# Two scratch buffers of their own and eight traced steps for the exponent tables of an S5 table builder

## The chip, the cores and the metric

The kernel runs on one core of one Trainium2 chip, as one launch. The metric is the device time of a run in microseconds (us). TensorE (PE) multiplies matrices, VectorE (DVE), ScalarE (ACT) and GpSimd (POOL) work elementwise, and SyncE (SP) issues nearly all DMA transfers, one after the other in the order of its queue: a transfer that has to wait for its data or its buffer holds back all behind it.

## The reference

The kernel computes two layers of a decoder trunk on x, 512 tokens by 1024. A layer is a feed-forward block, a mixer and a second feed-forward block, each between two RMS norms and modulated by a vector made from c. The mixer has gated delta heads and an S5 part. Shortened:

```python
for l in range(2):
    sh1, sc1, gt1, sh2, sc2, gt2, sh3, sc3, gt3 = split(silu(c) @ w_mod[l] + b_mod[l], 9)
    h = modulate(rms_norm(x, ff1_norm_pre[l]), sh1, sc1)
    x = x + 0.5 * gt1 * rms_norm(swiglu(h, ff1_w_in[l], ff1_w_out[l]), ff1_norm_post[l])
    h = modulate(rms_norm(x, mix_norm_pre[l]), sh2, sc2)
    x = x + gt2 * rms_norm(hybrid_mixer(h, ...), mix_norm_post[l])
    h = modulate(rms_norm(x, ff2_norm_pre[l]), sh3, sc3)
    x = x + 0.5 * gt3 * rms_norm(swiglu(h, ff2_w_in[l], ff2_w_out[l]), ff2_norm_post[l])
# S5, per group of 16 channels: a complex diagonal state of 64
abar = exp(dt * min(a_re, -1e-4)) * (cos(dt * a_im) + i sin(dt * a_im))   # dt = exp(log_dt)
x_t = abar * x_(t-1) + bbar * u_t;   y_t = real(c * x_t) + d * u_t
```

The kernel doesn't step the recurrence token by token. It makes tables of powers of the unit-modulus part of abar (er real, ei imaginary, 128 powers for each state) and of the input and output matrices, per layer and for four chunks of channels (4 groups of 128 rows in each table).

## The kernel before, in words

**Weights.** They come from HBM in units of 512 KB (128x1024; DMA on L216, named w0_35 for layer 0, unit 35) into a ring of four raw buffers. Each unit is split on chip into a high and a low half: ScalarE casts (L223, `wh`), VectorE subtracts (L231, `wl`), and three matmuls replace one (L266 to L268 into the hidden layer, tiles f00i, f02i, f10i, f12i; L273 to L275 out of it, f00o and so on: f00 is layer 0's first feed-forward block, f02 its second). A feed-forward block runs in three passes over its 22 hidden tiles: 7, 7 and 8. After a pass its hidden tiles are multiplied out into eight accumulators; L569 adds those of pass 1 on VectorE to the partial sums (f00pt). The second four of these accumulators live in the same PSUM pool as the hidden layer's, so that pass 2 cannot begin on TensorE until L569 has read one.

**The arena.** wh, wl, hidden activations, tables and partial sums all take slots of one pool, 71 buffers of 128x512 in rotation (`slot`, L65); a new tile waits until the last reader of its slot is done.

**Background work.** While a feed-forward block runs, two generators are stepped by a counter at each weight unit (`tick`, L193). `gen_mod` loads a part of w_mod into a raw buffer of the same ring (wm0_53, DMA on L141) and multiplies it on VectorE (L143). `gen_prep` builds the S5 tables, layer 0's beside f00 and layer 1's beside f02. `spread` divides each generator's number of steps over 40 units; for gen_prep it is `NPREP` (L828), 109.

**The table builder.** For each of four chunks (pr00 to pr03, and pr10 to pr13) gen_prep loads parameters (`params`, L692, tile bc, one buffer), computes on GpSimd the input table w, a masked copy (c0r, c0n), the output table c, and then the exponent tables er and ei by doubling: in step i of seven, the 2^i powers at hand are multiplied by the 2^i-th power, which gives the next 2^i (L804 to L818, the products through `pmul`, L679). y1 and y2 hold the products. `close` (L696) then transposes w (L703, pr02mb) and multiplies it (L708, L709, pr02g) on TensorE, and stores everything to a scratch in HBM through SP (L720, L754; er on L725, ei on L726). It runs as part of the next chunk's steps and waits while a pass is being multiplied out. VectorE has one small instruction per chunk, pr03dd (L788), that reads bc.

Order on each engine is that of the trace of the program, except where waits are given: every `yield` of gen_prep is a place where its instructions and the block's own meet, so the number of yields and the rate set which instruction stands before which on every engine.

Of the kernel before, what the change touches and what calls it, by code (L numbers as in the profile page):

```python
# [7 lines left out]
F32 = mybir.dt.float32  # L8
# [3 lines left out]
ALU = mybir.AluOpType  # L12
# [3 lines left out]
P = 128  # L16
# [38 lines left out]
def trunk(ctx: ExitStack, tc: tile.TileContext, x_d, c, wmod, wun, vecs, wab, s5p, cst_d, out, depth=2):  # L55
    nc = tc.nc
    PE, ACT, DVE, POOL = nc.tensor, nc.scalar, nc.vector, nc.gpsimd
# [8 lines left out]
    pw_p = ctx.enter_context(tc.tile_pool(name="prep", bufs=1))  # L66
# [4 lines left out]
    def slot(name, dt=F32):  # L71
        return ar_p.tile([P, T], dt, tag="ar", name=name)

    def small(n, name):
        return sm_p.tile([P, n], F32, tag=f"s{n}", name=name, bufs=NSMALL[n])
# [7 lines left out]
    def q4(t):  # L83
        return t.rearrange("p (c i) -> p c i", c=4)

    def col(t, n):
        return t.rearrange("p (a b) -> p a b", b=1).to_broadcast([P, t.shape[1], n])
# [22 lines left out]
    def rest():  # L110
        behind(nc.scalar.dma_start(out=cst[:, 2 * P:], in_=cst_d[:, 2 * P:]))
        POOL.tensor_copy(identr, ident)
        POOL.tensor_copy(sufr, suf)
        POOL.tensor_copy(negr, cst[:, C_NEG:C_NEG + P])
# [23 lines left out]
    def gen_mod(l, tiles):  # L138
        for n in tiles:
            w = raw_p.tile([P, 1024], F32, tag="raw", name=f"wm{l}_{n}")  # L140
            nc.sync.dma_start(out=w, in_=wmod[l, n])  # L141
            m = small(1, f"ma{l}_{n}")
            DVE.scalar_tensor_tensor(w, w, 1.0, cb, op0=ALU.mult, op1=ALU.mult, accum_out=m)  # L143
            DVE.tensor_tensor(mod[l][:, n:n + 1], m, vec[l][:, V_BMOD + n:V_BMOD + n + 1], op=ALU.add)
            yield
# [43 lines left out]
    def spread(units, **gens):  # L189
        bg.extend([g, n / units, 0.0] for g, n in gens.values())  # L190
# [111 lines left out]
    def new_h(name):  # L302
        return [(slot(f"{name}h{k}", F32R), slot(f"{name}l{k}", F32R)) for k in range(KD)]
# [181 lines left out]
    def ff(l, s, h):  # L485
# [22 lines left out]
        for p, (j0, j1) in enumerate(PASSES):  # L508
            nk = j1 - j0
            js = list(range(j0, j1))  # L510
            if p == 0 and l == 0 and s == 0:
# [5 lines left out]
                rest()  # L517
                spread(40, mod=(gen_mod(0, range(16, 72)), 56), prep=(gen_prep(0), NPREP))
            elif p == 0:
# [55 lines left out]
    def gen_prep(l):  # L575
# [3 lines left out]
        def tiny(nm):  # L579
            return pw_p.tile([P, 16], F32, tag="t" + nm, name=f"t{nm}{l}")  # L580
# [15 lines left out]
        def cm(nm, ar, ai, br, bi):  # L596
            orr, oi = tiny(nm + "r"), tiny(nm + "i")
            mul(t1, ar, br)
            mul(t2, ai, bi)
            sub(orr, t1, t2)  # L600
            mul(t1, ar, bi)
            mul(t2, ai, br)
            add(oi, t1, t2)
            return orr, oi
# [11 lines left out]
        kq, r, z, s, c2, m, ck, sk = [tiny(n) for n in ("kq", "rr", "z", "s", "c", "m", "ck", "sk")]  # L616
# [50 lines left out]
        e = cm("e2", ur, ui, ur, ui)  # L667
        en = [cm("e4", *e, *e)]
# [9 lines left out]
        def pmul(o, a, b):  # L678
            POOL.tensor_tensor(o, a, b, op=ALU.mult)  # L679
# [10 lines left out]
        def params(ch):  # L690
            t = pw_p.tile([P, 384], F32, tag="bc", name=f"pr{l}{ch}bc")
            behind(nc.sync.dma_start(out=t, in_=s5p[l, :, 48 + 384 * ch:432 + 384 * ch]))  # L692
            return t
# [37 lines left out]
        for ch in range(4):  # L731
            qs = slice(4 * ch, 4 * ch + 4)

            def a2(v):
                return col(v[:, qs], 16)

            def q3(v):
                return v.rearrange("p (q h) -> p q h", h=16)

            def part_h(off):  # L740
                return q3(bc[:, off:off + 64])

            def at(v, t):
                return v.rearrange("p (q t h) -> p t q h", q=4, t=4)[:, t]

            def gmask(o, v):
                pmul(o.rearrange("p (q g h) -> p q g h", q=4, g=2),
                     v.rearrange("p q (a h) -> p q a h", a=1).to_broadcast([P, 4, 2, 16]),
                     gm.rearrange("p (a g b) -> p a g b", a=1, b=1).to_broadcast([P, 4, 2, 16]))

            def diag(i, src, ch=ch):
                for g in range(2):
                    v = dram[ch, 64 * g:64 * g + 64, i * T:i * T + T].rearrange("p (q g n) -> p q g n", q=4, g=2)
                    nc.sync.dma_start(out=v[:, :, g], in_=src(g))  # L754

            nm = f"pr{l}{ch}"
            h1 = q3(pw_p.tile([P, 64], F32, tag="k1", name=nm + "k1"))
            h2 = q3(pw_p.tile([P, 64], F32, tag="k2", name=nm + "k2"))

            def step(o_r, o_i, i_r, i_i, m_r, m_i):  # L760
                pmul(h1, i_r, m_r)
                pmul(h2, i_i, m_i)
                POOL.tensor_tensor(o_r, h1, h2, op=ALU.subtract)
                pmul(h1, i_r, m_i)
                pmul(h2, i_i, m_r)
                POOL.tensor_tensor(o_i, h1, h2, op=ALU.add)

            w = slot(nm + "w")
            wr, wi = w[:, 0:256], w[:, 256:512]
            br, bi = part_h(S_BRE), part_h(S_BIM)  # L770
            step(at(wr, 3), at(wi, 3), br, bi, a2(fr), a2(fi))
            yield
            for t in (2, 1, 0):
                step(at(wr, t), at(wi, t), at(wr, t + 1), at(wi, t + 1), a2(a1r), a2(a1i))
                yield
            if rest is not None:
                yield from rest
            c0r = pw_p.tile([P, P], F32, tag="c0r", name=nm + "c0r")
            c0n = pw_p.tile([P, P], F32, tag="c0n", name=nm + "c0n")
            cin = q3(pw_p.tile([P, 64], F32, tag="cin", name=nm + "cin"))  # L780
            gmask(c0r, part_h(S_CRE))
            POOL.tensor_scalar(cin, part_h(S_CIM), -1.0, None, op0=ALU.mult)
            gmask(c0n, cin)
            for _ in range(2):
                yield
            dd = small(P, nm + "dd")
            qg = lambda v: v.rearrange("p (q g h) -> p q g h", q=4, g=2)
            DVE.tensor_tensor(qg(dd[32:64]), qg(bc[32:64, S_D2:S_D2 + P]),  # L788
                              ident[32:64, 48:64].rearrange("p (a b h) -> p a b h", a=1, b=1)
                              .to_broadcast([32, 4, 2, 16]), op=ALU.mult)  # L790
            yield
            yield
            c = slot(nm + "c")
            cr, cn = c[:, 0:256], c[:, 256:512]
            for t in range(4):
                i_r, i_i = (part_h(S_CRE), cin) if t == 0 else (at(cr, t - 1), at(cn, t - 1))
                step(at(cr, t), at(cn, t), i_r, i_i, a2(a1r), a2(nai))
                yield
                if t == 1 and ch < 3:
                    bc = params(ch + 1)  # L800
            er, ei = slot(nm + "er"), slot(nm + "ei")
            POOL.memset(q4(er)[:, :, 0:1], 1.0)
            POOL.memset(q4(ei)[:, :, 0:1], 0.0)
            y1, y2 = slot(nm + "y1"), slot(nm + "y2")  # L804
            for i in range(7):
                n = 1 << i
                z1 = y1[:, :4 * n].rearrange("p (q n) -> p q n", q=4)
                z2 = y2[:, :4 * n].rearrange("p (q n) -> p q n", q=4)
                b_r, b_i = col(en[i][0][:, qs], n), col(en[i][1][:, qs], n)
                lo_r, lo_i = q4(er)[:, :, 0:n], q4(ei)[:, :, 0:n]  # L810
                pmul(z1, lo_r, b_r)
                pmul(z2, lo_i, b_i)
                POOL.tensor_tensor(q4(er)[:, :, n:2 * n], z1, z2, op=ALU.subtract)
                pmul(z1, lo_r, b_i)
                pmul(z2, lo_i, b_r)
                POOL.tensor_tensor(q4(ei)[:, :, n:2 * n], z1, z2, op=ALU.add)
                if i > 3:
                    yield  # L818
            y1 = y2 = z1 = z2 = None
            rest = close(ch, nm, w, c, er, ei, c0r, c0n, dd, qg, diag)  # L820
            w = c = er = ei = wr = wi = cr = cn = c0r = c0n = dd = v = None
            yield
# [2 lines left out]
        yield from rest  # L825

    s5r, s5d, neg = {}, {}, {}
    NPREP = 15 + 4 * 20 + 14  # L828

    def gen_s5(l, utc, res, nm0, chunks):  # L830
        for ch in chunks:
# [688 lines left out]
    h = new_h("h0")  # L1520

    for l in range(depth):
        if l:
            spread(40, mod=(gen_mod(l, range(32, 72)), 40))
        h = ff(l, 0, h)
        drain()
        h = mixer(l, h)
        if l + 1 < depth:
            load_vec(l + 1)
            spread(40, mod=(gen_mod(l + 1, range(32)), 32), prep=(gen_prep(l + 1), NPREP))  # L1530
        h = ff(l, 2, h)
        drain()
# [105 lines left out]
```

## Time and profile before

| | us |
|---|---|
| median of 3 runs | 2133.61 |
| lowest, highest | 2125.81, 2135.41 |
| profiled execution: its own time | 2130.65 |
| span in its profile | 2128.8 |
| TensorE busy | 2040.2 (96% of the span) |
| VectorE, ScalarE, GpSimd busy | 1248.4, 891.9, 489.0 |
| mean granted clock of TensorE, share of full speed | 0.981 |

Times within the span count from its start. The span is the time between the first and the last instruction; the rest of an execution's time lies around it. Busy time overlaps among engines, so that only one engine's idle time can be set against the span. A wait in brackets behind an instruction is the idle time of its engine just before it, and what ended that.

### The profile page before, as it was taken

To read this page: it belongs to the slowest core of one execution; us is meant where nothing else is said; L and a number is where in the kernel's file an instruction comes from. 1 tells how busy PE (TensorE), PEld (TensorE's weight loads), DVE (VectorE), ACT (ScalarE), POOL (GpSimd) and SP (SyncE) were. 2 spreads that over 40 slices of the span, in tenths; PEclk is the share of its full clock that TensorE was granted. 3 is DMA by queue.
4 is the path that set the end of the run, shared out by engine and by line. 5 is a ranking of instruction groups with operands and counts; after the bars stand their busy time and mean duration, and the time that the engine had idled before them with its cause. 6 is when DMAs were issued, how large, how long until landed. Compare 5 with 4: busy or idle time off the path is not lost.

```text
span 2128.8 us, 31850 instructions
## 1 busy us (share of the span) xinstructions
PE 2040.2 (96%) x11702; PEld 1732.1 (81%) x11702; DVE 1248.4 (59%) x2936; ACT 891.9 (42%) x1956; POOL 489.0 (23%) x925
## 2 busy tenths in 40 slices
PE   7999979999999999989999999999989899999998
PEld 5888768798778988868889888888978789888886
DVE  8965556856666864455584456558485575324235
ACT  5532213564567633222363322236637674323132
POOL 4167860211321036663010000001122200000001
PEclk9999989999999999989999999999999899999999
DMA  7776666303311435556423555552142132223231
GB/s 291 234 254 218 208 193 216 109 31 129 116 46 70 149 104 160 169 165 181 153 90 119 165 171 188 162 165 80 30 168 71 41 100 90 93 95 129 70 99 50
DMA packets 109696, 286.07 MB, mean 134 GB/s; under 512 B 31154, under 2 KB 32610, under 8 KB 109540
## 3 DMA queue, kind: packets, MB, share of 16 engines
q1 hardware_dynamic: 108388, 282.39, 40.5%
q8 instruction: 92, 1.51, 0.3%
q10 hardware_dynamic: 1152, 1.65, 0.2%
q14 instruction: 64, 0.52, 0.1%
HBM read 267.59 MB, written 16.41 MB: 133 GB/s over the span
## 4 chain that ended last, share of the span: by engine, by line
PE 72%; DVE 12%; DMA 5%; ACT 4%; issue 3%; POOL 3%; SPq 0%; DVEq 0%; POOLq 0%; ACTq 0%
PE f10i L266 4%; PE f10i L268 4%; PE f10i L267 4%; PE f00i L266 3%; PE f00i L267 3%; PE f12i L268 3%; PE f12i L266 3%; PE f00i L268 3%; PE f12i L267 3%; DMA wm<-in_wmod 3%; PE f02i L266 2%; PE f02i L268 2%; PE f02i L267 2%; DVE wl L231 2%; PE f10o L274 1%
## 5 line engine op out<-in xcount | busy, mean ns | idle before, releaser
L231 DVE TENSOR_TENSOR wl<-w,wh 128x512 fp32r<-128x512 f32 x608 | 408.8, 725 | 105.7 <-ACT wh L223 92.0
L223 ACT CAST wh<-w 128x512 fp32r<-128x512 f32 x648 | 356.7, 617 | 96.6 <-DMA w<-in_wun 50.8
L143 DVE SCALAR_TENSOR_TENSOR wm<-wm,cb 128x1024 f32<-128x1024 f32 x128 | 158.9, 1242 | 224.7 <-DMA wm<-in_wmod 224.6
L266 PE MATMUL f02i<-m0ohh,wh 128*128 128x512 f32 (+1 forms) x416 | 149.7, 362 | 7.9 <-DVE f02pt L569 6.6
L266 PE MATMUL f10i<-f02ohh,wh 128*128 128x512 f32 (+1 forms) x416 | 150.0, 360 | 1.9 <-DVE f02pt L324 1.6
L267 PE MATMUL f10i<-f02ohl,wh 128*128 128x512 f32 (+1 forms) x416 | 148.9, 358 | 2.1 <-ACT f02ohl L404 2.1
L266 PE MATMUL f00i<-h0h,wh 128*128 128x512 f32 x344 | 134.5, 397 | 16.2 <-DVE f00pt L569 12.3
L267 PE MATMUL f02i<-m0ohl,wh 128*128 128x512 f32 (+1 forms) x416 | 149.1, 359 | 0.0
L268 PE MATMUL f02i<-m0ohh,wl 128*128 128x512 f32 (+1 forms) x416 | 148.8, 359 | 0.2 <-DVE wl L231 0.2
L266 PE MATMUL f12i<-m1ohh,wh 128*128 128x512 f32 (+1 forms) x416 | 148.0, 358 | 0.8 <-ACT f12sg L498 0.8
L268 PE MATMUL f10i<-f02ohh,wl 128*128 128x512 f32 (+1 forms) x416 | 148.8, 358 | 0.0
L267 PE MATMUL f12i<-m1ohl,wh 128*128 128x512 f32 (+1 forms) x416 | 148.1, 357 | 0.0
L268 PE MATMUL f12i<-m1ohh,wl 128*128 128x512 f32 (+1 forms) x416 | 147.8, 357 | 0.2 <-DVE wl L231 0.2
L267 PE MATMUL f00i<-h0l,wh 128*128 128x512 f32 x344 | 136.5, 397 | 0.9 <-DVE h0l L1493 0.9
L268 PE MATMUL f00i<-h0h,wl 128*128 128x512 f32 x344 | 135.9, 395 | 0.0
L330 POOL TENSOR_TENSOR f12pt<-f12pt,Gr 128x512 f32<-128x512 f32 x8 | 10.5, 1314 | 403.1 <-ACT scr L329 403.1
L499 DVE TENSOR_TENSOR f12sg<-f12sg,f12i 128x512 f32<-128x512 f32 (+1 forms) x26 | 15.7, 605 | 136.8 <-PE f12i L268 120.8
L266 PEld LDWEIGHTS f02i<-m0ohh,wh 128*128 128x128 f32 x416 | 78.9, 190 | 20.0 <-issue 6.7
L330 POOL TENSOR_TENSOR f10pt<-f10pt,Gr 128x512 f32<-128x512 f32 x8 | 10.7, 1337 | 361.0 <-ACT scr L329 357.2
L266 PEld LDWEIGHTS f10i<-f02ohh,wh 128*128 128x128 f32 x416 | 79.2, 190 | 13.7 <-DVE f02pt L324 1.8
L266 PEld LDWEIGHTS f00i<-h0h,wh 128*128 128x128 f32 x344 | 65.4, 190 | 30.8 <-issue 12.4
L267 PEld LDWEIGHTS f10i<-f02ohl,wh 128*128 128x128 f32 x416 | 79.2, 190 | 13.6 <-ACT f02ohl L404 2.4
(2597 smaller groups left out, 5245.2 us busy)
## 6 DMA issues: line engine op xcount, KB each, us to landing
w<-in_wun SPq DMA_DIRECT2D x324, 512.0 KB, 4.0
wm<-in_wmod SPq DMA_DIRECT2D x128, 512.0 KB, 4.7
wm<-in_wmod SPq DMA_DIRECT2D x32, 256.0 KB, 5.8
s5d<-zero SPq DMA_DIRECT2D x4, 1280.0 KB, 14.6
Gr<-Gd SPq DMA_DIRECT2D x12, 256.0 KB, 3.4
x<-in_x SPq DMA_DIRECT2D x4, 512.0 KB
m0s0tb<-s5d SPq DMA_DIRECT2D x7, 256.0 KB
m0s1tb<-s5d SPq DMA_DIRECT2D x7, 256.0 KB, 4.7
```

Of the source, the lines that this page charges most:

```text
L143: DVE.scalar_tensor_tensor(w, w, 1.0, cb, op0=ALU.mult, op1=ALU.mult, accum_out=m)
L223: ACT.copy(hi[j], raw[:, j * T:j * T + T])
L231: e.tensor_tensor(lo[j], raw[:, j * T:j * T + T], hi[j].bitcast(F32), op=ALU.subtract)
L266: PE.matmul(ps, hi, h[0][:, sl], start=start, stop=False)
L267: PE.matmul(ps, hi, h[1][:, sl], start=False, stop=False)
L268: mark["pe"] = PE.matmul(ps, lo, h[0][:, sl], start=False, stop=stop)
L274: PE.matmul(ps, gh, lo, start=False, stop=False)
L330: (POOL if self.part else DVE).tensor_tensor(y, src, self.G[dh], op=ALU.mult)
L499: DVE.tensor_tensor(sg, sg, pu[:, :n], op=ALU.mult)
```

## The change

y1 and y2 become two tiles of 128x128 with a buffer of their own each, in the pool `prep`, in place of two arena slots of 128x512. So that they suffice, the last doubling step (i=6) works on two of the four groups at a time: twelve GpSimd instructions of 128x128 products in place of six of 128x256. The steps end after i=0, 1, 3, 4, 5 and each half of 6, and once more as before: eight in place of four per chunk, and NPREP goes from 109 to 125, so that more steps are made at each weight unit.

```diff
--- before.py
+++ after.py
@@ -801,21 +801,22 @@
             er, ei = slot(nm + "er"), slot(nm + "ei")
             POOL.memset(q4(er)[:, :, 0:1], 1.0)
             POOL.memset(q4(ei)[:, :, 0:1], 0.0)
-            y1, y2 = slot(nm + "y1"), slot(nm + "y2")
+            y1, y2 = [pw_p.tile([P, P], F32, tag=f"y{i}", name=f"{nm}y{i}") for i in range(2)]
             for i in range(7):
                 n = 1 << i
-                z1 = y1[:, :4 * n].rearrange("p (q n) -> p q n", q=4)
-                z2 = y2[:, :4 * n].rearrange("p (q n) -> p q n", q=4)
-                b_r, b_i = col(en[i][0][:, qs], n), col(en[i][1][:, qs], n)
-                lo_r, lo_i = q4(er)[:, :, 0:n], q4(ei)[:, :, 0:n]
-                pmul(z1, lo_r, b_r)
-                pmul(z2, lo_i, b_i)
-                POOL.tensor_tensor(q4(er)[:, :, n:2 * n], z1, z2, op=ALU.subtract)
-                pmul(z1, lo_r, b_i)
-                pmul(z2, lo_i, b_r)
-                POOL.tensor_tensor(q4(ei)[:, :, n:2 * n], z1, z2, op=ALU.add)
-                if i > 3:
-                    yield
+                for h in ((slice(0, 2), slice(2, 4)) if i == 6 else (slice(0, 4),)):
+                    m = h.stop - h.start
+                    z1, z2 = [y[:, :m * n].rearrange("p (q n) -> p q n", q=m) for y in (y1, y2)]
+                    b_r, b_i = [col(e[:, 4 * ch + h.start:4 * ch + h.stop], n) for e in en[i]]
+                    lo_r, lo_i = q4(er)[:, h, 0:n], q4(ei)[:, h, 0:n]
+                    pmul(z1, lo_r, b_r)
+                    pmul(z2, lo_i, b_i)
+                    POOL.tensor_tensor(q4(er)[:, h, n:2 * n], z1, z2, op=ALU.subtract)
+                    pmul(z1, lo_r, b_i)
+                    pmul(z2, lo_i, b_r)
+                    POOL.tensor_tensor(q4(ei)[:, h, n:2 * n], z1, z2, op=ALU.add)
+                    if i != 2:
+                        yield
             y1 = y2 = z1 = z2 = None
             rest = close(ch, nm, w, c, er, ei, c0r, c0n, dd, qg, diag)
             w = c = er = ei = wr = wi = cr = cn = c0r = c0n = dd = v = None
@@ -825,7 +826,7 @@
         yield from rest
 
     s5r, s5d, neg = {}, {}, {}
-    NPREP = 15 + 4 * 20 + 14
+    NPREP = 15 + 4 * 24 + 14
 
     def gen_s5(l, utc, res, nm0, chunks):
         for ch in chunks:
```

The number of instructions grows by 48 on GpSimd (6 for each of eight chunks) and is the same on every other engine, where the order changes. Three places follow. In the rows w_35_2302 is unit 35 of the weights (the last number is only the tile's), and wm_43 a part of w_mod.

SP's queue, layer 0, around the stores of pr01er and pr01ei. Before:

```order
L141 DMA wm_42_2234<-in_wmod 128x1024
L754 DMA s5d<-pr01c 64x4x64 x2
L216 DMA w_35_2302<-in_wun 128x1024
L141 DMA wm_43_2312<-in_wmod 128x1024
L141 DMA wm_44_2317<-in_wmod 128x1024
L725 DMA s5d<-pr01er 128x512
L726 DMA s5d<-pr01ei 128x512
L216 DMA w_36_2378<-in_wun 128x1024
L141 DMA wm_45_2388<-in_wmod 128x1024
L720 DMA s5d<-pr01gs 16x64 x2
```

And now:

```order
L216 DMA w_34_2236<-in_wun 128x1024
L754 DMA s5d<-pr01c 64x4x64 x2
L141 DMA wm_42_2246<-in_wmod 128x1024
L725 DMA s5d<-pr01er 128x512
L726 DMA s5d<-pr01ei 128x512
L216 DMA w_35_2314<-in_wun 128x1024
L141 DMA wm_43_2324<-in_wmod 128x1024
L141 DMA wm_44_2329<-in_wmod 128x1024
L216 DMA w_36_2390<-in_wun 128x1024
L141 DMA wm_45_2400<-in_wmod 128x1024
```

The two stores have moved ahead of w_35, wm_43 and wm_44. Further on pr03bc moves from behind w_40, w_41 and three stores of pr02c to a place ahead of w_40; around the stores of pr02er and pr02ei nothing moves.

VectorE, layer 0, at the end of f00's pass 1, where f00gl_2377 and w_38 are operands of the multiplication out of the hidden layer. Before:

```order
L159 SCALAR_TENSOR_TENSOR G_1_4828<-mod_124,vec_122 128x8
L499 TENSOR_TENSOR f00sg_2478<-f00sg_2478,f00i_2453 128x512
L501 TENSOR_TENSOR f00gl_2377<-f00sg_2478,f00gh_2376 128x512
L231 TENSOR_TENSOR wl_0_2493<-w_38_2487,wh_0_2489 128x512
L231 TENSOR_TENSOR wl_1_2494<-w_38_2487,wh_1_2490 128x512
L231 TENSOR_TENSOR wl_0_2527<-w_39_2521,wh_0_2523 128x512
L231 TENSOR_TENSOR wl_1_2528<-w_39_2521,wh_1_2524 128x512
L788 TENSOR_TENSOR pr03dd<-pr03bc,cst 32x128
L231 TENSOR_TENSOR wl_0_2561<-w_40_2555,wh_0_2557 128x512
```

And now:

```order
L159 SCALAR_TENSOR_TENSOR G_1_4852<-mod_124,vec_122 128x8
L788 TENSOR_TENSOR pr03dd<-pr03bc,cst 32x128
L499 TENSOR_TENSOR f00sg_2498<-f00sg_2498,f00i_2473 128x512
L501 TENSOR_TENSOR f00gl_2389<-f00sg_2498,f00gh_2388 128x512
L231 TENSOR_TENSOR wl_0_2513<-w_38_2507,wh_0_2509 128x512
L231 TENSOR_TENSOR wl_1_2514<-w_38_2507,wh_1_2510 128x512
L231 TENSOR_TENSOR wl_0_2547<-w_39_2541,wh_0_2543 128x512
L231 TENSOR_TENSOR wl_1_2548<-w_39_2541,wh_1_2544 128x512
L231 TENSOR_TENSOR wl_0_2581<-w_40_2575,wh_0_2577 128x512
```

pr03dd, which reads pr03bc, has moved ahead of f00sg, f00gl and the units 38 and 39.

TensorE, layer 0, between pass 1 (f00o) and pass 2 (f00i) of f00. Before:

```order
L274 MATMUL f00o_2618<-wl_1_2578,f00gh_2376 128x512
L275 MATMUL f00o_2618<-wh_1_2574,f00gl_2377 128x512
L162 MATMUL Gp_0_2836<-cst,G_0_2834 8x128
L703 MATMUL pr02mb_2877<-cst,pr02w 64x128 x4
L703 MATMUL pr02mb_2883<-cst,pr02w 64x128 x4
L708 MATMUL pr02g<-pr02c0r,pr02w 64x32
L709 MATMUL pr02g<-pr02c0n,pr02w 64x32
L708 MATMUL pr02g<-pr02c0r,pr02w 64x32
L709 MATMUL pr02g<-pr02c0n,pr02w 64x32
```

And now (the rows of f00i at the top are the end of the first hidden tile's first unit in pass 2):

```order
L266 MATMUL f00i_2893<-h0h_119,wh_1_2654 128x512
L267 MATMUL f00i_2893<-h0l_120,wh_1_2654 128x512
L268 MATMUL f00i_2893<-h0h_119,wl_1_2658 128x512
L703 MATMUL pr02mb_2940<-cst,pr02w 64x128 x4
L703 MATMUL pr02mb_2946<-cst,pr02w 64x128 x4
L708 MATMUL pr02g<-pr02c0r,pr02w 64x32
L709 MATMUL pr02g<-pr02c0n,pr02w 64x32
L708 MATMUL pr02g<-pr02c0r,pr02w 64x32
L709 MATMUL pr02g<-pr02c0n,pr02w 64x32
```

The small matmuls of pr02 stood before the first matmul of pass 2 and now stand behind its first 24.

## Rows read from the trace of the kernel before

**Rows 1.** The page's first part: busy time, share of the span and instructions.

```profile
PE 2040.2 (96%) x11702; PEld 1732.1 (81%) x11702; DVE 1248.4 (59%) x2936; ACT 891.9 (42%) x1956; POOL 489.0 (23%) x925
```

**Rows 2.** Busy time by stretch: PE, PEld, DVE, ACT, POOL; then TensorE clock, DMA share, GB/s.

```profile
240.00:260.00 20.00, 20.00 (x90) 16.57 (x89) 12.26 (x23) 2.28 (x4) 17.23 (x42) 1.00 0.72 241
260.00:280.00 20.00, 4.00 (x34) 3.27 (x33) 8.75 (x18) 4.42 (x9) 18.12 (x42) 0.69 0.53 160
280.00:300.00 20.00, 20.00 (x79) 16.37 (x80) 10.71 (x18) 3.91 (x7) 17.45 (x53) 0.89 0.47 146
940.00:960.00 20.00, 10.42 (x49) 8.26 (x48) 13.33 (x25) 3.43 (x8) 11.78 (x30) 0.67 0.51 168
```

**Rows 3.** The waits: total us, times, longest.

```profile
ACT wh L223 <- POOL pr02ei L816: 15.6, 1, 15.6
...
ACT wh L223 <- POOL pr12ei L816: 13.2, 1, 13.2
```

**Rows 4.** Timeline of TensorE, 255 to 285: start, length, what ran, [idle before].

```profile
261.63 0.27 PE L162 MATMUL Gp<-cst,G 128*8 128x128 f32 x1
261.74 1.03 PE L703 MATMUL pr02mb<-cst,pr02w 128*64 128x128 f32 x8
266.46 0.27 PE L708 MATMUL pr02g<-pr02c0r,pr02w 128*64 128x32 f32 x2 [3.69 <-DVE f00pt L569]
...
267.27 0.28 PE L709 MATMUL pr02g<-pr02c0n,pr02w 128*64 128x32 f32 x2
279.87 0.77 PE L266 MATMUL f00i<-h0h,wh 128*128 128x512 f32 x1 [12.31 <-DVE f00pt L569]
```

**Rows 5.** Timeline of VectorE, 256 to 285.

```profile
264.23 1.49 DVE L231 TENSOR_TENSOR wl<-w,wh 128x512 fp32r<-128x512 f32 x2 [8.78 <-ACT wh L223]
...
269.50 1.22 DVE L143 SCALAR_TENSOR_TENSOR wm<-wm,cb 128x1024 f32<-128x1024 f32 x1 [1.63 <-DMA wm<-in_wmod]
...
277.69 1.23 DVE L143 SCALAR_TENSOR_TENSOR wm<-wm,cb 128x1024 f32<-128x1024 f32 x1 [3.51 <-DMA wm<-in_wmod]
...
279.04 2.47 DVE L569 TENSOR_TENSOR f00pt<-f00pt,f00o 128x512 f32<-128x512 f32 x4
```

**Rows 6.** Timeline of SP's DMA queue, 255 to 285.

```profile
261.51 0.33 SPq L725 DMA_DIRECT2D s5d<-pr02er  x1
...
265.74 2.29 SPq L141 DMA_DIRECT2D wm<-in_wmod  x2
...
274.02 0.33 SPq L141 DMA_DIRECT2D wm<-in_wmod  x1
```

**Rows 7.** Timeline of GpSimd, 225 to 285.

```profile
240.85 0.33 POOL L679 TENSOR_TENSOR pr03k<-pr03bc,tfr 128x64 f32<-128x64 f32 x1 [4.00 <-DMA pr03bc<-in_s5p]
...
256.74 0.40 POOL L679 TENSOR_TENSOR pr02y<-pr02er,te128r 128x128 f32<-128x128 f32 x1
...
259.48 0.61 POOL L679 TENSOR_TENSOR pr02y<-pr02er,te256r 128x256 f32<-128x256 f32 x1
...
263.50 0.32 POOL L763 TENSOR_TENSOR pr03w<-pr03k,pr03k 128x64 f32<-128x64 f32 x1
```

**Rows 8.** Timeline of SP's DMA queue, 920 to 960.

```profile
928.74 0.33 SPq L726 DMA_DIRECT2D s5d<-pr12ei  x1
929.15 0.38 SPq L216 DMA_DIRECT2D w<-in_wun  x1
```

**Rows 9.** Timeline of TensorE, 935 to 960.

```profile
955.04 0.77 PE L266 MATMUL f02i<-m0ohh,wh 128*128 128x512 f32 x1 [6.61 <-DVE f02pt L569]
```

**Rows 10.** Timeline of SP's DMA queue, 195 to 252.

```profile
202.87 0.33 SPq L216 DMA_DIRECT2D w<-in_wun  x1
...
220.70 0.53 SPq L216 DMA_DIRECT2D w<-in_wun  x1
```

**Rows 11.** Timeline of VectorE, 225 to 256.

```profile
226.94 1.50 DVE L231 TENSOR_TENSOR wl<-w,wh 128x512 fp32r<-128x512 f32 x2
...
240.74 0.28 DVE L788 TENSOR_TENSOR pr03dd<-pr03bc,cst 32x128 f32<-32x128 f32 x1 [5.72 <-DMA pr03bc<-in_s5p]
```

## The prediction

> **What bounds the kernel now.** I read the page first: TensorE is busy for 2040.2 of the span's 2128.8 us [rows 1], so at most 88.6 us are idle and a change pays only where TensorE stands still, or where it makes it stand still. Next came the busy time by stretches of 20 us. TensorE fills nearly every one (20.00), and around the table builder two do not: 4.00 us in 260 to 280, with a granted clock of 0.69, and 10.42 in 940 to 960, with 0.67 [rows 2]. I call them stall A (layer 0) and stall B (layer 1). Then the waits: ScalarE's cast L223 waits 15.6 us once for GpSimd's pr02ei on L816, and 13.2 us once for pr12ei [rows 3]. The casts want an arena slot that the doubling's scratch y1 or y2 still holds. These waits look like the whole story; the timelines say less.
>
> In stall A TensorE finishes f00o at 261.63, does two pieces of small table matmuls (pr02mb 1.03 us, pr02g 0.8 from its first start to its last) and starts f00i14 at 279.87, after 12.31 us for L569 [rows 4]. VectorE's own rows show what L569 stood behind: wl44 after 8.78 us for the cast, then four modulation products L143, of which the later ones wait for their loads wm (1.63 us, and 3.51 the last), then L569 at 279.04 [rows 5]. Why are the loads late? The DMA queue of SP is in order: the store of pr02er leaves at 261.51, w0_46 behind it, wm0_53 and wm0_54 from 265.74 (into a raw buffer that wl44 frees), then the store of pr02ei, w0_47 and, at 274.02, wm0_55 [rows 6]. So two things hold stall A, and both end with GpSimd's doubling: the slot (pr02ei complete at 263.5) and the store that blocks SP (pr02er, which it takes up at 261.51) [rows 6, 7].
>
> In stall B the slot's wait ends at 928.7, but SP stands at the store of pr12ei until 928.74 too, and issues w0_138 at 929.15 only [rows 8]. TensorE resumes at 955.04, after 6.61 us for L569 [rows 9]. The slot and the queue are released by one and the same instruction.
>
> **The change, part by part.** *Own buffers.* The waits of L223 and L231 for pr02ei and pr12ei go. What is late next is SP. In stall A, wl44 no longer comes after the doubling, so wm0_53 and wm0_54 follow the store of pr02er at once instead of 4.2 us later (265.74 less 261.51). From there I repeat the old pace. A load is consumed 3.7 us after its issue (274.02 to 277.69 [rows 5, 6]), and a product with its readout takes 1.3. Call T the end of pr02er. wm0_53 is issued at T+0.8, its product runs from 4.5 to 5.8, wm0_54's from there to 7.1, wm0_55 is issued at 7.2, its product ends at 12.2, and one L569 later (0.95 us from the product's end to 279.87) f00i14 starts, at T+13.2. Before, 279.87−261.51=T+18.4. That is −5.2 us if T stays.
>
> *T itself.* The doubling step i=5 takes 259.48−256.74=2.74 us for six 128x128 operations, step i=6 263.50−259.48=4.02 for six of 128x256 [rows 7]. Two halves of i=6 cost 2x2.74, +1.46 per chunk. pr02er's last write was the third of six (261.51−259.48=2.0 us into the step) and is now the ninth of twelve (4.1): +2.1. The chunk before is on the way too: +1.46. Against this, pr03bc is now loaded before w0_40 instead of after it, w0_41 and three stores, so GpSimd's wait of 4.00 us for it [rows 7] can go entirely. Sum −0.4. pr02bc moves ahead of wm0_39, worth up to about a load's 3.7 us earlier, while more of pr01's doubling stands behind it: I bound this by ±4 and take T about 1 us earlier in all, the sum's side. f00i14 then starts at 260.5+13.2=273.7 instead of 279.87, −6.2.
>
> *Matmuls that move.* pr02mb and pr02g stood inside the stall, where they cost nothing. In the new order they follow f00i14's first unit, whose cover is gone: 1.03+0.8=+1.8 [rows 4]. **Stall A: −4.4 us**, between −8 and 0.
>
> *Stall B.* The order around pr12 is as before. SP still stops at pr12er and pr12ei, whose doubling ends 1.46 us later, and everything from w0_138 to 955.04 follows. Taking away ACT's and VectorE's wait gives nothing, since the next operand is still to be issued. **+1.5 us**, between −3 (wl137 earlier frees a buffer that is used early) and +2.
>
> *SP's order.* The stores of pr01er and pr01ei now precede w0_35 to w0_37 instead of following w0_35. w0_35 left at 202.87 and will wait for pr01ei, about 213; w0_37 left at 220.70 and I put it at about 227.6 [rows 10]. It is needed when f00o's fifth row of pass 1 begins, at 261.63−120x0.222=235.0 (120 matmuls before its end, 90 of them in 20.00 us [rows 2]). Its wl followed its issue by 7.7 us before (220.70 to 228.44 [rows 10, 11]), so 235.3: at the edge. *pr03dd* on VectorE, which waited 5.72 us for pr03bc [rows 11], now stands ahead of f00sg13, f00gl13 and wl38, which TensorE needs about 235.8. pr03bc then lands near 237 and wl38 is ready near 239.5: a new stall of some 4 us. I cost it at nothing, because it only moves f00o's end from 261.6 towards 266, and stall A ends at 273.7 whatever f00o does. If stall A were gone, these 4 us would count in full. The same move in pr00 and in layer 1's pr10, pr11 and pr13 puts stores in front of loads that ran about 10 us ahead; zero, between 0 and +2. The 48 additional GpSimd instructions otherwise lie beside matmuls.
>
> Sum: −4.4+1.5+0=−2.9 on the profiled execution's own 2130.65 (span 2128.8 plus 1.9 around it), 2127.8. That execution lies 3.0 under the median of 2133.61, so the median comes to about 2131.
>
> A page of the Trainium skill argues for more. "Perfetto Trace Analysis", section Optimization Strategy, says that a repeated gap on the engine that should be saturated can mean too little SBUF for the next tile. By it both stalls would be gaps of the arena. The rows agree that a slot is waited for [rows 3], and show beside it a queue that is released at the same moment [rows 6, 8]. By the page the sum would be the first rival's time below, by the rows the one above.
>
> **Rivals.** *The slots were the cause.* If the arena alone made the loads late, since slots free the raw buffers and so SP, the whole run of loads moves forward. Stall A's 12.31+3.69 and stall B's 6.61 of waiting go [rows 4, 9], and with them the clock's loss (0.69 and 0.67 in these stretches). The rows for it are the waits [rows 3]; against it stand SP's stores, which wait for GpSimd in any order [rows 6, 8]. Price: −16 (A alone) to −27 (A, B, and 2 us each for matmuls that come back slowly: 79 start in the 20 us after stall A instead of 90 [rows 2]). About 2112.
>
> *Stores before weights* (the other side). Each microsecond by which pr03bc or pr01's tables come later delays T and f00sg13 by one. SP reaches pr03bc only after w0_35 to w0_39, whose issue hangs on pr01ei. From T of about 264.9, 3.4 us above today's (the 5.2 gained less 1.8), each further microsecond is one on the time. With pr03bc landing at 252 instead of 240.7, T is near 273, f00i14 near 286: +6 there, +1.8 matmuls, +1.5 in B and 2 to 5 from starved passes in layer 1: +11 to +14, about 2146. For it: SP's order and 17 to 18 us of work in every 20 on GpSimd [rows 2]. Against: w0_37's load had 6 us in hand before (ready 228.44, needed 235.0).
>
> *Nothing moves.* If T grows by the 3.4, A is unchanged, and the time is the old one within B's +1.5: 2135.
>
> **How the numbers follow.** The forecast, a small gain, 0.47, with its own range 2125 to 2137. Slots the cause 0.22, nothing moves 0.14, stores before weights 0.17. About 10.7 us (0.5%) can be told from no change here. Faster by more takes the first rival and a little of the forecast: 0.24. Slower by more takes the second: 0.16. Within: 0.60. For 8 in 10 the range takes half of each outer rival: 2113 to 2145.
>
> **What would show it.** In the changed profile the waits for pr02ei and pr12ei are gone; SP's store of pr02er leaves near 260.5 with wm0_53 right behind; f00i14 starts near 274 with pr02mb after its first unit; VectorE waits for pr03bc near 232 to 237 and f00o has a gap there; f02i14 of layer 1 starts some 13 us after f02o's end, as now. I am wrong if SP's stores of pr02er and pr12er leave 5 us or more from there, or if 940 to 960 fills up.

## The result, and the profile after

The changed kernel takes 2146.28 us (median of 5 runs, 2142.01 to 2148.05) against 2131.86 of the kernel before beside it. The ratio is 1.0065, with a 95% interval of 1.005 to 1.008: slower by some 14 us, where about 2131 had been forecast. Its profiled execution took 2146.28 us with a span of 2144.5, 15.7 more than the one of before.

First the page's line of busy time, which answers to [rows 1]:

```profile
PE 2045.4 (95%) x11702; PEld 1733.0 (81%) x11702; DVE 1243.4 (58%) x2936; ACT 892.0 (42%) x1956; POOL 509.4 (24%) x973
```

TensorE has the same 11702 matmuls in 5 us more (the mean granted clock is 0.977 instead of 0.981), so some 10 us of the 15.7 are idle time. Then the stretches of 20 us that answer to [rows 2]:

```profile
200.00:220.00 20.00, 18.44 (x96) 15.02 (x94) 7.45 (x15) 3.34 (x7) 17.75 (x44) 1.00 0.35 109
220.00:240.00 20.00, 9.51 (x32) 7.29 (x33) 11.48 (x20) 5.81 (x11) 18.02 (x41) 0.66 0.63 196
260.00:280.00 20.00, 16.75 (x75) 13.54 (x73) 10.38 (x20) 2.40 (x5) 18.06 (x39) 0.99 0.50 172
280.00:300.00 20.00, 9.10 (x32) 7.25 (x32) 9.08 (x18) 1.33 (x3) 6.23 (x15) 0.58 0.55 183
```

There are two holes beside layer 0's tables now, a new one from 218 to 230, and stall A, which has moved from 262 to 280 to 276 to 291. TensorE's timeline, the first matmul after each hole, and after stall B (for [rows 4, 9]):

```profile
230.49 0.79 PE L266 MATMUL f00i<-h0h,wh 128*128 128x512 f32 x1 [12.05 <-ACT wh L223]
```

```profile
290.90 0.76 PE L266 MATMUL f00i<-h0h,wh 128*128 128x512 f32 x1 [14.15 <-DVE f00pt L569]
```

```profile
969.89 0.76 PE L266 MATMUL f02i<-m0ohh,wh 128*128 128x512 f32 x1 [6.40 <-DVE f02pt L569]
```

f00i14, with which pass 2 of f00 begins, starts at 290.90 instead of 279.87, +11.0. f02i14, the same place in f02 (the second block of layer 0, beside which layer 1's tables are built; the prediction calls it layer 1), starts at 969.89 instead of 955.04, +14.9. Nearly all of the loss is there. SP's queue, around the stores of pr01 and of pr02 (for [rows 6, 10]):

```profile
204.36 0.33 SPq L141 DMA_DIRECT2D wm<-in_wmod  x1
218.33 0.33 SPq L725 DMA_DIRECT2D s5d<-pr01er  x1
219.70 0.33 SPq L726 DMA_DIRECT2D s5d<-pr01ei  x1
220.13 0.37 SPq L216 DMA_DIRECT2D w<-in_wun  x1
```

```profile
275.65 0.33 SPq L725 DMA_DIRECT2D s5d<-pr02er  x1
276.03 0.42 SPq L216 DMA_DIRECT2D w<-in_wun  x1
276.56 0.87 SPq L141 DMA_DIRECT2D wm<-in_wmod  x2
...
284.54 0.33 SPq L141 DMA_DIRECT2D wm<-in_wmod  x1
```

SP issues nothing between 204.7 and 218.33: it stands at the store of pr01er. w0_35 leaves at 220.13 instead of 202.87. The store of pr02er leaves at 275.65 instead of 261.51. GpSimd's waits for the parameters and for the slot of pr02ei (for [rows 7]), and VectorE's for the loads behind SP's stops (for [rows 5]):

```profile
196.06 0.39 POOL L679 TENSOR_TENSOR pr02k<-pr02bc,tfr 128x64 f32<-128x64 f32 x1 [11.62 <-DMA pr02bc<-in_s5p]
```

```profile
247.30 0.33 POOL L679 TENSOR_TENSOR pr03k<-pr03bc,tfr 128x64 f32<-128x64 f32 x1 [4.23 <-DMA pr03bc<-in_s5p]
...
251.83 0.10 POOL L803 MEMSET pr02ei<- 128x4 f32 x1 [3.57 <-DMA s5d<-pr02c]
```

```profile
226.09 1.23 DVE L143 SCALAR_TENSOR_TENSOR wm<-wm,cb 128x1024 f32<-128x1024 f32 x1 [15.69 <-DMA wm<-in_wmod]
```

```profile
281.94 1.23 DVE L143 SCALAR_TENSOR_TENSOR wm<-wm,cb 128x1024 f32<-128x1024 f32 x1 [10.98 <-DMA wm<-in_wmod]
...
288.73 1.23 DVE L143 SCALAR_TENSOR_TENSOR wm<-wm,cb 128x1024 f32<-128x1024 f32 x1 [4.02 <-DMA wm<-in_wmod]
...
290.08 2.48 DVE L569 TENSOR_TENSOR f00pt<-f00pt,f00o 128x512 f32<-128x512 f32 x4
```

### The profile page after: what moved, and what is told of

Read it like the earlier page. It is cut to its first block, busy times and chain, and to the rows that moved or that the text cites. A ratio compares the mean times of both kernels' runs of the same rounds, so it can differ in the third digit from the quotient of the medians.

```text
span 2144.5 us, 31901 instructions
## 1 busy us (share of the span) xinstructions
PE 2045.4 (95%) x11702; PEld 1733.0 (81%) x11702; DVE 1243.4 (58%) x2936; ACT 892.0 (42%) x1956; POOL 509.4 (24%) x973
## 4 chain that ended last, share of the span: by engine, by line
PE 62%; DVE 14%; DMA 8%; POOL 6%; issue 4%; ACT 4%; SPq 1%; DVEq 0%; POOLq 0%; ACTq 0%
DMA wm<-in_wmod 5%; PE f10i L266 4%; PE f10i L267 4%; PE f10i L268 4%; PE f12i L268 3%; PE f12i L266 3%; PE f12i L267 3%; DVE wl L231 2%; PE f02i L266 2%; PE f02i L268 2%; PE f02i L267 2%; PE f00i L266 1%; PE f00i L268 1%; PE f00i L267 1%; PE f12o L273 1%
## 5 line engine op out<-in xcount | busy, mean ns | idle before, releaser
L231 DVE TENSOR_TENSOR wl<-w,wh 128x512 fp32r<-128x512 f32 x608 | 405.7, 720 | 99.8 <-ACT wh L223 98.4
L223 ACT CAST wh<-w 128x512 fp32r<-128x512 f32 x648 | 356.8, 618 | 109.9 <-DMA w<-in_wun 75.6
L499 DVE TENSOR_TENSOR f12sg<-f12sg,f12i 128x512 f32<-128x512 f32 (+1 forms) x26 | 15.7, 606 | 136.8 <-PE f12i L268 120.8
```

The lines of the kernel that those rows point to most:

```text
L223: ACT.copy(hi[j], raw[:, j * T:j * T + T])
L231: e.tensor_tensor(lo[j], raw[:, j * T:j * T + T], hi[j].bitcast(F32), op=ALU.subtract)
L499: DVE.tensor_tensor(sg, sg, pu[:, :n], op=ALU.mult)
```

## The experiments

Two numbers are followed through all of them: T, the end of pr02er on GpSimd, and the start of f00i14 on TensorE. Both are read from one profiled execution of each kernel. A third is the ratio to the kernel before run beside each kernel.

| kernel | scratch | last doubling | steps | bc loads | T | f00i14 | f00i14 − T | ratio, 95% interval |
|---|---|---|---|---|---|---|---|---|
| before | arena | 6 | 4 | SP | 261.5 | 279.87 | 18.4 | |
| e6_own_unsplit | own | 6 | 4 | SP | 261.5 | 277.24 | 15.7 | 0.9992 [0.9981, 1.0004] |
| e9_split_arena | arena | 12 | 4 | SP | 266.0 | 283.88 | 17.9 | 1.0060 [1.0041, 1.0079] |
| e1_four_steps | own | 12 | 4 | SP | 268.6 | 283.57 | 15.0 | 1.0043 [1.0027, 1.0059] |
| e2_eight_steps_arena | arena | 6 | 8 | SP | 267.8 | 286.93 | 19.1 | 1.0032 [1.0020, 1.0045] |
| e12_own_unsplit_eight | own | 6 | 8 | SP | 269.3 | 284.45 | 15.2 | 1.0017 [1.0005, 1.0028] |
| after | own | 12 | 8 | SP | 275.6 | 290.90 | 15.3 | 1.0065 [1.0050, 1.0080] |
| e10_after_bc | own | 12 | 8 | GpSimd | 266.4 | 281.73 | 15.3 | 0.9963 [0.9951, 0.9975] |
| e8_before_bc | arena | 6 | 4 | GpSimd | 251.9 | 270.95 | 19.0 | 0.9913 [0.9898, 0.9928] |
| e7_own_unsplit_bc | own | 6 | 4 | GpSimd | 254.2 | 269.79 | 15.6 | 0.9905 [0.9890, 0.9920] |

**Order or work?** Two kernels take the change apart: one has the four steps back, the other has only the eight steps.

```diff
 # e1_four_steps, against the changed kernel
-                    if i != 2:
+                    if i > 3 and h.stop == 4:
                         yield
-    NPREP = 15 + 4 * 24 + 14
+    NPREP = 15 + 4 * 20 + 14
 # e2_eight_steps_arena, against the kernel before
-                if i > 3:
+                if i != 2:
+                    yield
+                if i == 6:
                     yield
-    NPREP = 15 + 4 * 20 + 14
+    NPREP = 15 + 4 * 24 + 14
```

> Own scratch buffers and the split last doubling stay; the steps are four per chunk again (NPREP 109), so that every engine but GpSimd has the order of the kernel before. Theory O (the eight steps' order does the harm: stores of pr01er and pr01ei ahead of w0_35 hold SP, and pr02's parameters come behind more of pr01's doubling): no stall near 218, SP's store of pr01er within 4 us of 208, f00i14 starts between 273 and 280, time 2126 to 2134. Theory W (the 48 additional GpSimd instructions, +1.46 us per chunk, make the tables late): the store of pr02er leaves 4 us or more after 261.5, f00i14 at 283 or later, time 2138 or more.

> The kernel before (scratch in the arena, last doubling in six instructions) with eight steps per chunk and NPREP 125: SP, TensorE and ScalarE have the order of the changed kernel. Theory O: the stall near 218 is there with about 12 us, time 2142 to 2152 (a little more than the changed kernel if the arena's waits for pr02ei add to it). Theory W: no such stall, time 2130 to 2137.

Neither theory held alone. e1 took 2140.51 us against 2130.45, as W says, with SP's and TensorE's order of before; e2 took 2136.17, a time that W allows, but with the early hole (the one near 218) that only O foresees, of 7.24 us instead of 12. SP's store and f00i14 in e1, and the two matmuls behind the holes of e2:

```profile
268.63 0.33 SPq L725 DMA_DIRECT2D s5d<-pr02er  x1
```

```profile
283.57 0.76 PE L266 MATMUL f00i<-h0h,wh 128*128 128x512 f32 x1 [19.12 <-DVE f00pt L569]
```

```profile
225.62 0.79 PE L266 MATMUL f00i<-h0h,wh 128*128 128x512 f32 x1 [7.24 <-ACT wh L223]
```

```profile
286.93 0.77 PE L266 MATMUL f00i<-h0h,wh 128*128 128x512 f32 x1 [14.38 <-DVE f00pt L569]
```

T is 7.1 us later in e1 and 6.3 later in e2; both together make 13.4, and the changed kernel has 14.1. f00i14 is later by 3.7 and 7.1, together 10.8; the changed kernel has 11.0. The parts add up, and they act through T.

**SP's stop at the stores.** Two kernels send er and ei through GpSimd's own queue: e3 is the changed kernel with this edit, e5 is e1 with it.

```diff
-            nc.sync.dma_start(out=dram[ch, :, 5 * T:6 * T], in_=er)
-            nc.sync.dma_start(out=dram[ch, :, 6 * T:7 * T], in_=ei)
+            nc.gpsimd.dma_start(out=dram[ch, :, 5 * T:6 * T], in_=er)
+            nc.gpsimd.dma_start(out=dram[ch, :, 6 * T:7 * T], in_=ei)
```

> The changed kernel with the stores of er and ei issued by GpSimd's own DMA queue, so that SP never waits for the doubling; orders are else the same but for a few swaps. If SP standing at these stores is the cause (theory O, its first half): w0_35 leaves near 204, the 12 us near 218 go, and most of the 14 us at f00i14 too, time 2112 to 2126. If instead GpSimd is late because pr02's parameters land late and its work lies behind that wait (second half), DVE's and TensorE's waits move to pr03bc and the slots: f00i14 near 285, time 2135 or more.

> Own scratch buffers, four steps, and the stores of er and ei on GpSimd's queue: both things that hold stalls A and B in the kernel before (slot, and SP behind the stores) are taken away, in its order. My reading of the two stalls: f00i14 starts by 268 instead of 279.87 and f02i14 by 947 instead of 955.04, time 2108 to 2120. If the modulation loads are late for another reason (the raw ring alone): f00i14 at 275 or later, time 2126 or more.

e3 took 2134.35 us (ratio 1.0016, 1.0006 to 1.0026). The early hole was gone, so SP's stop at pr01er had made it; and T was 264.6, 11 us earlier, with 2.39 us for pr02bc instead of 11.62, as SP now reached that load sooner. But f00i14 still started at 284.85, as the second half of its expectation had it. e5 missed by 15 us: 2135.39 (1.0017, 1.0005 to 1.0029), with f00i14 at 287.27. TensorE's row in e3, and VectorE's row in e5, which shows what took SP's place:

```profile
284.85 0.76 PE L266 MATMUL f00i<-h0h,wh 128*128 128x512 f32 x1 [20.76 <-DVE f00pt L569]
```

```profile
269.18 0.71 DVE L231 TENSOR_TENSOR wl<-w,wh 128x512 fp32r<-128x512 f32 x1 [11.35 <-DMA s5d<-pr02er]
```

wl44, the other half of the unit whose cast waited for y1 or y2 before, now waits for an arena slot that the store of pr02er frees (10.35 us in e3). The raw buffers wait with it: w0_46 leaves at 271.39 in e5, when wl44 is done. er and ei lie in the arena too, so that one wait for a slot is followed by the next. In e5 y1 and y2 are out of the arena and SP is free; what is left is the last of three waits that end with the same doubling.

**Scratch, split and steps one by one.** e6 has own scratch alone: one buffer of 128x256, the second product going straight into its place; e9 the split of the last doubling alone (the changed loop, y1 and y2 from the arena, steps and NPREP of before); e12 is e6 with the eight steps of e2.

```diff
 # e9_split_arena, against the changed kernel (with the steps of e1_four_steps)
-            y1, y2 = [pw_p.tile([P, P], F32, tag=f"y{i}", name=f"{nm}y{i}") for i in range(2)]
+            y1, y2 = slot(nm + "y1"), slot(nm + "y2")
 # e6_own_unsplit, against the kernel before
-            y1, y2 = slot(nm + "y1"), slot(nm + "y2")
+            y1 = pw_p.tile([P, 2 * P], F32, tag="y0", name=f"{nm}y0")
...
-                pmul(z2, lo_i, b_i)
-                POOL.tensor_tensor(q4(er)[:, :, n:2 * n], z1, z2, op=ALU.subtract)
+                pmul(hi_r, lo_i, b_i)
+                POOL.tensor_tensor(hi_r, z1, hi_r, op=ALU.subtract)
```

> The kernel before with one scratch buffer of its own (128x256 floats, the second product goes straight into its place in er or ei), four steps, the last doubling in six instructions: own scratch alone, without the split and without the eight steps. Theory S (the split's additional GpSimd time, added up chunk after chunk, is what e1_four_steps lost): the store of pr02er leaves at 260 to 264 and f00i14 starts 15 us after it, at 275 to 279; time 2124 to 2132. If own scratch itself costs (the slots turn in another order), f00i14 is at 281 or later and the time 2136 or more.

> The split alone: scratch in arena slots, four steps, the last doubling in twelve instructions. Theory S: pr02er is done near 268 as in e1_four_steps, f00i14 starts 18 to 19 us later, at 286 to 288, f02i14 about 2 us later again than that shift; time 2138 to 2145, the worst of the four with four steps. If the split costs nothing: 2128 to 2134.

> The changed kernel without the split: one scratch buffer of its own (128x256), the last doubling in six instructions, eight steps; SP, TensorE, VectorE and ScalarE have exactly the order of the changed kernel. If split and eight steps add up: pr02er is done near 268 as in e2_eight_steps_arena, the stall near 218 to 226 has 6 to 8 us, f00i14 starts 15 to 16 us after pr02er, at 282 to 285, time 2130 to 2138, half of the changed kernel's loss. If the eight steps do all of the harm: 2142 or more, with 11 us or more near 218. If the split does all: 2125 to 2130.

The three came out as expected, but that e9's T was 266.0 instead of 268, and its f00i14 2 us earlier with it; its f02i14 (964.12) lay 9 us behind that of before, 5 more than f00i14, where 2 more were expected. Own scratch alone: 2127.56 us, f00i14 2.6 us earlier at the same T, in all no more than the measurement can tell. Split alone: 2140.44. Own scratch and eight steps: 2133.96, with an early hole of 6.71 us. From e12 to the changed kernel the split is added (and the one scratch buffer becomes two), and on every engine but GpSimd the order is the same: 1.0017 to 1.0065, some 10 us. So the split costs 10 to 13 us with eight steps as with four (e6 to e1, 0.9992 to 1.0043; e9 alone, 1.0060), and the eight steps about 5 (e6 to e12). SP's store and f00i14 in e6, and the two matmuls behind the holes of e12:

```profile
261.56 0.33 SPq L725 DMA_DIRECT2D s5d<-pr02er  x1
```

```profile
277.24 0.77 PE L266 MATMUL f00i<-h0h,wh 128*128 128x512 f32 x1 [13.20 <-DVE f00pt L569]
```

```profile
225.04 0.79 PE L266 MATMUL f00i<-h0h,wh 128*128 128x512 f32 x1 [6.71 <-ACT wh L223]
```

```profile
284.45 0.77 PE L266 MATMUL f00i<-h0h,wh 128*128 128x512 f32 x1 [13.09 <-DVE f00pt L569]
```

How long does the split step take? The last doubling step took 6.1, 5.0 and 4.1 us in chunks 0 to 2 before, and 7.6, 8.2 and 5.4 in e1: 6.0 us more in all, where three times 1.46 would be 4.4. In the changed kernel it took 5.43 in each of the three, and in e12, without the split, 3.95: there the split cost no more than its own work. GpSimd's rows of the first of these in e1, and VectorE's:

```profile
155.02 0.40 POOL L679 TENSOR_TENSOR pr00y<-pr00er,te256r 128x128 f32<-128x128 f32 x1
155.38 1.44 POOL L679 TENSOR_TENSOR pr00y<-pr00ei,te256i 128x128 f32<-128x128 f32 x1
...
157.43 0.40 POOL L679 TENSOR_TENSOR pr00y<-pr00er,te256i 128x128 f32<-128x128 f32 x1
```

```profile
155.33 1.23 DVE L143 SCALAR_TENSOR_TENSOR wm<-wm,cb 128x1024 f32<-128x1024 f32 x1 [1.75 <-DMA wm<-in_wmod]
```

The same product takes 0.40 us, and 1.44 where it meets a modulation product of VectorE's; it ends 0.26 us after that one. "SBUF — State Buffer", section SBUF: two separate sides, of the Trainium skill says that VectorE, with two inputs from SBUF, and GpSimd share a pair of ports as an exclusive lock for a whole instruction. The rows agree; no run here took VectorE's work away to show it.

**How the chunks hang together.** A longer doubling in one chunk reaches the next through SP's queue, where bc stands behind the stores of er and ei of the chunk before. SP's rows in the kernel before, and in e1:

```profile
157.20 0.33 SPq L725 DMA_DIRECT2D s5d<-pr00er  x1
...
188.44 0.38 SPq L692 DMA_DIRECT2D pr02bc<-in_s5p  x1
```

```profile
161.32 0.33 SPq L725 DMA_DIRECT2D s5d<-pr00er  x1
...
191.02 0.38 SPq L692 DMA_DIRECT2D pr02bc<-in_s5p  x1
```

The stores of pr00er and pr00ei leave 4.1 and 2.3 us later in e1, and pr02bc 2.6; those of pr01 4.8 and 4.2, and pr03bc 3.1. The one buffer of bc is not what holds the load: in e1 GpSimd had read pr01bc for the last time at 173.7.

**The chain on GpSimd.** If T is what counts, GpSimd's waits for bc should be worth as much as its work. They are taken out by loading bc through GpSimd's queue:

```diff
-            behind(nc.sync.dma_start(out=t, in_=s5p[l, :, 48 + 384 * ch:432 + 384 * ch]))
+            behind((nc.gpsimd if ch else nc.sync).dma_start(out=t, in_=s5p[l, :, 48 + 384 * ch:432 + 384 * ch]))
```

> The kernel before with only the bc loads moved to GpSimd's queue. If GpSimd's chain sets the stalls: pr02er's store by 253, f00i14 by 275 (the slot of y1 and y2 holds it 3 us longer than own scratch), time 2108 to 2122. If not: 2126 or more.

> As e6_own_unsplit, and the parameters bc of chunks 1 to 3 are loaded through GpSimd's own DMA queue instead of SP's, behind the instructions that free the buffer. If GpSimd's chain from one chunk to the next sets the stalls: its waits for pr02bc and pr03bc (7.9 and 4.0 us) shrink to under 3 us together, the store of pr02er leaves by 253, stall A is under 10 us and f00i14 starts by 272; in layer 1 the waits for pr12bc and pr13bc (8.7, 16.7) go and f02i14 starts 8 to 13 us earlier; time 2106 to 2120. If the chain isn't what sets them, 2126 or more.

> The changed kernel with the bc loads of chunks 1 to 3 on GpSimd's queue; split and eight steps stay. If the chain on GpSimd is what both act through: the wait of 11.6 us for pr02bc goes, pr01er is done by 210 and SP's store of it no longer starves TensorE near 218, pr02er is done by 264, f00i14 starts by 279; time 2112 to 2126. If the eight steps hurt by SP's order alone, w0_35 still leaves 8 us or more later than in the kernel before, the stall near 218 stays, time 2130 or more.

> e7_own_unsplit_bc with the stores of er and ei on GpSimd's queue as well, four steps: nothing of the tables holds SP. Where the slots of er and ei are what is left (as the 11.35 us for the store of pr02er in e5_four_steps_pool_stores), f00i14 starts 13 to 18 us after pr02er, no earlier than in e7 (269.8), time 2106 to 2113. If SP's stop at the stores was still the larger part, f00i14 starts by 266 and the time is 2100 to 2106.

e8 took 2110.89 us, e7 2108.58, e10 2122.44: the change of one queue gains some 18 us on the kernel before (0.9913) and 22 on the changed one (1.0065 to 0.9963). In e10 the wait for pr02bc went from 11.6 to 0.98 us, pr01er was done at 209.1, and the early hole shrank to 2.41; the split and the eight steps are still in it, and T (266.4) and f00i14 came 2.5 us after the bounds I had set. In e10 w0_35 still left at 212.05, 9.2 us later than before, as the other expectation had it, but neither the long hole nor the time that it tied to this came. The rows of e7: GpSimd's issue of pr03bc and its wait for it, which did not go as expected, SP's store, a little after the 253 expected, and f00i14.

```profile
224.72 0.59 POOL L692 DMA_DIRECT2D pr03bc<-in_s5p  x1
230.14 0.72 POOL L679 TENSOR_TENSOR pr03k<-pr03bc,tfr 128x64 f32<-128x64 f32 x1 [4.83 <-DMA pr03bc<-in_s5p]
```

```profile
254.24 0.33 SPq L725 DMA_DIRECT2D s5d<-pr02er  x1
```

```profile
269.79 0.77 PE L266 MATMUL f00i<-h0h,wh 128*128 128x512 f32 x1 [4.88 <-DVE f00pt L569]
```

On GpSimd's queue pr03bc is issued as the last instruction ahead of its own first use, so that GpSimd waits for the whole load, though the buffer had been read for the last time at 213.35. Beside f02 the wait for pr13bc fell from 16.66 us before to 3.40, and f02i14 started without a wait of over 1 us, at 936.44 instead of 955.04, more than the 8 to 13 us expected: stall B is gone. e11, with the stores on GpSimd's queue as well, took 2112.96 us (0.9921, 0.9903 to 0.9940): no better than e7, the slot of er again (VectorE waits 9.39 us for its store). That is the first of the two expectations, but f00i14, at 275.29, came 21.7 us after T, as in e5, and not 13 to 18. e7 beats both kernels, by 0.95% and 1.6%.

## Why the prediction was wrong

**The step that failed is T.** The prediction put it at 260.5, "about 1 us earlier in all"; it came at 275.6, so that f00i14, forecast 6.2 us earlier, came 11.0 later. By the table, the eight steps moved T by 7.8 us (e6 to e12) and the split by 6.3 (e12 to the changed kernel). Of its terms, "GpSimd's wait of 4.00 us for it can go entirely" was wrong: pr03bc is loaded earlier in SP's order but not in time, as SP itself was late (the load left at 243.34, and before at 237.84), and the wait was 4.23. "pr02bc ... up to about a load's 3.7 us earlier": it came 3.4 later (196.06 against 192.68, GpSimd's first use of it), and with the wait of 11.62 us standing two instructions into pr01's doubling, that doubling (done at 211.3 before, 219.7 now) lay behind it nearly whole. A term that it lacked: at the first write into pr02ei GpSimd stood 3.57 us for an arena slot, until a store of SP's had landed; the kernel before, e1, e6 and e9 have no such wait there, e2 has 2.37 us and e12 4.42. And the split was counted as 1.46 us for the chunk before and 2.1 for its own. It adds up over every chunk, since bc stands in SP's queue behind stores that wait for the doubling, so that the waits move with the work instead of absorbing it: they were 11.3, 7.7 and 3.9 us in e1, against 11.50, 7.86 and 4.00. The bound of ±4 was too narrow for a chain of three chunks. The sign of being wrong came: the stores of pr02er and pr12er left 14 and 16 us later than before (pr12er at 942.5).

**Own buffers: right in kind, too large.** The waits of L223 and L231 for pr02ei and pr12ei went, and what was late next was SP, as said. f00i14 came at T+15.3 instead of T+13.2: wm0_53 and wm0_54 were issued together with w0_46, and the first was taken up 5.4 us after its issue (276.56 to 281.94) instead of 3.7. In the pairs of the table own scratch gains 2.7 (e6), 2.9 (e1) and 3.9 us (e12), not 5.2.

**SP's order: wrong by 7 to 9 us.** w0_35 was put at 213 and left at 220.13; w0_37 at 227.6 and left at 236.61. I weighed the weight units and not wm0_43 and wm0_44, which stand behind the stores too and whose products stand ahead of f00sg on VectorE: it waited 15.69 us, and TensorE 12.05, in a hole that begins some 17 us ahead of the place I watched (235.8). That a hole there costs nothing by itself fits the runs: with 6.71 us (e12) and 12.05 f00i14 comes the same 15 us after T, and in e3, with none, 20.

**Stall B: close.** +1.5 was forecast, between −3 and +2; f02i14 came 15.1 us after the last matmul of f02o (954.83), 12.9 before (942.13): +2.2. The moved matmuls ran behind f00i14's first unit, as said (pr02mb at 299.17); what they cost there no run shows.

**The rivals.** "Stores before weights" named the time (2146) and its place, SP ahead of w0_35, and gave T 273 and f00i14 286; they were 275.6 and 290.9. It had 0.17, against 0.47 for a gain. What it lacked is the split's share, 10 of some 15 us by e12. That its total fits is luck in part: it had +6 at f00i14, where 11.0 came, and 2 to 5 us from starved passes further on, where the time from f00i14 to the last matmul of f02o grew by 1.7. "The slots were the cause" fell with e6: 0.9992, where it had −16 to −27 us. The sentence of the Trainium skill, "Perfetto Trace Analysis", section Optimization Strategy, that a repeated gap can mean too little SBUF would have misled here: the slot was waited for, and buying it gave 2.6 us.

What stays open: what an earlier issue of pr03bc on GpSimd's queue would gain (4.83 us of waiting in e7), and what GpSimd's meetings with VectorE cost in all; neither was tried.

## What to carry to other kernels

When several waits end with the same instruction, taking one away only brings up the next; find the chain that sets that instruction's time and shorten it (here six parameter loads of 0.2 MB each on another queue, for 0.9%). Background work that is split into more, smaller instructions to save buffers lengthens such a chain in every round, and a wait inside the chain doesn't absorb it if the wait is released by the chain itself, here by a load that stands behind the chain's own stores. In a queue kept in order, look at everything behind a store that waits for slow work, the small loads too.

## What the runs showed of the hardware

The same 128x128 product on GpSimd took 0.40 us alone and 1.44 beside a VectorE instruction of 1.23 (e1). DMAs issued by GpSimd cost its own queue 0.6 us each here (0.61 and 0.56 in e5), and a load of 0.2 MB issued there landed 5.3 us after its issue (pr03bc in e7).
